# Hybrid decoder layer on one core: a written order for the first tile, readers of a PSUM bank grouped by engine, means on ScalarE, stores one step later

## The chip, the cores and the metric

The kernel runs on 1 core of a Trainium2 chip. The metric is the device time of one execution in microseconds (us). A core has five engines that each take their instructions in order and wait for one another by semaphores: TensorE (PE, matmuls and transposes), VectorE (DVE), ScalarE (ACT), GpSimd (POOL) and SyncE (SP), which here only issues DMAs. Matmuls write to PSUM; all other tiles lie in SBUF.

## The reference

One decoder layer on x of 1024 rows (tokens) by 1024 columns, all in float32:

```python
h = rms_norm(x, norm_mix_pre)
proj = h @ w_in                      # columns: u, v (256 each), then q, k, v of 12 heads (64 each)
a_out = spatial_gating(u, v, ...)    # gelu, layer norm of v, causal 128-row mix, times u
b_out = dilated_attention(q, k, v, rel_bias)
x = x + rms_norm(concat(a_out, b_out) @ w_out, norm_mix_post)
h = rms_norm(x, norm_ffn_pre)
g = gelu(causal_dwconv(h @ w_gate, conv_w, conv_b))
y = (g * (h @ w_up)) @ w_down        # 2816 inner columns
x = x + rms_norm(y, norm_ffn_post)
```

A norm is `x * rsqrt(mean(x*x) + eps) * gain`. In the kernel each is a sum of squares on ACT, a mean plus eps, the power −0.5 on POOL, and a multiplication on DVE.

## The kernel before

Rows are worked in 8 tiles of 128. Every matrix product in float32 is made of three passes with split operands: an operand is written as hi (a rounded copy) and lo (operand minus hi), and PE adds hi·hi, hi·lo and lo·hi. So each operand costs a copy (L77 on DVE, L73 on ACT; both are `split`) and a subtraction (L78, on DVE or POOL), and the names end in h and l: whuv and wluv are the weights for the columns u and v, hTh and hTl the transposed normed x, whv and wlv the first weights for the heads' v.

The stages, with their times in the profile:

- 0 to 25 us, the start: load of tile 0, its norm (`norm_x`), its transposes (`trans_x`, xT in PSUM), the split of four pieces of weight.
- to 75 us, the uv projection: for each tile 24 matmuls (`proj_a`), the transposes of the next tile in the middle of them (`mid`), and the gate's norm (`uv_a` to `uv_d`: tm, mu, mm, s, vnl). Between them the weights of the first head group are split (`split_w("v0", ...)`, for i = 3 to 6).
- to 148 us, the projections for the heads' v (`v_out`: hi on ACT, lo on DVE from a PSUM bank) and the gate's product.
- to 463 us, 12 heads. Projections of later heads (L479) fill PE between logits (s), softmax rows (row), transposes (pt, with the splits pth on ACT and ptl on DVE) and products with V (o). Late in it the finished columns of the first row tile are split for w_out (`mix_split`, tiles ms).
- to 552 us, w_out: for each tile in the order 0, 1, 2, 3, 4, 6, 5, 7 a product of 48 matmuls, then `wout_end` (squares, mean in two halves by `rstd_half`, norm, sum with x, and a second norm with `rstd_of`). The transposes of a finished tile (`h2_trans`, L728) stand on PE behind the product of the next one. Its eight scaled copies (L733, stg) and further splits (hs) are ACT's and DVE's.
- to 975 us, the gate and up products by a Strassen-Winograd scheme, with the convolution and gelu.
- to 1198 us, the down projection, in the same scheme: seven products, the steps (n, p), each with 11 pieces p. For every step an s tile is loaded (`sf`, L945) and split. In the last product (n = 4) the even row tiles are normed and stored (`final`, L1037 and L1038) while the odd ones are worked; the last five pieces are done for one odd tile after the other (the tail). L1059 is the add that ends a tile there, L1008 its square, L1023 its mean (n4m), L1025 its power.

The orders of PE and SP are as the code is written. DVE, ACT and POOL are ordered by a scheduler at build time, which places an instruction by its expected readiness, so the written order binds there only by its dependencies.

## Time and profile before

| what | value |
|---|---|
| median of 3 runs | 1198.22 us (1197.21 to 1200.38) |
| the profiled execution's own time | 1199.82 us |
| its span | 1198.1 us |
| PE busy | 1163.6 us, 97% |
| DVE, ACT, POOL busy | 839.7, 582.9, 370.6 us |
| PE idle | 34.5 us |

A row of the timeline has the start in us, the duration in us, the engine, the line, the operation and what it writes and reads; in brackets stands the idle time of the engine just before it and what ended that. Rows that follow each other with the same form are merged, with their count behind an x. The profile's lines are numbers of the kernel before; the kernel after has others (L1088 is the add of the tail, for instance).

### The profile page before, as it was taken

How to read it: one execution, taken by the hardware profiler on the slowest of the kernel's cores; microseconds unless marked ns; L12 is line 12 of the kernel's file. 1: busy time of each engine (PE TensorE's matmuls, PEld its weight loads, DVE VectorE, ACT ScalarE, POOL GpSimd, SP SyncE). 2: the span in 40 equal slices, each digit the busy share in tenths (PEclk: the TensorE clock that was granted, in tenths of full speed). 3: DMA queues.
4: the chain of work that ended last, by engine and by line, in shares of the span. 5: the costliest groups of instructions: out<-in, count | busy, mean ns of one | idle time of the engine just before them, and what ended most of it. 6: DMA issues, size and time to landing. Idle time of an engine off the chain costs nothing.

```text
span 1198.1 us, 16554 instructions
## 1 busy us (share of the span) xinstructions
PE 1163.6 (97%) x5691; PEld 976.8 (82%) x5691; DVE 839.7 (70%) x1559; ACT 582.9 (49%) x1174; POOL 370.6 (31%) x402
## 2 busy tenths in 40 slices
PE   7899999999999999999999999999999999999996
PEld 5789978888887878887788888888888888888884
DVE  5752257777777775468997678777777679779665
ACT  5532256667765664457534243432434345446521
POOL 2850023334323374234033313332133310000451
PEclk9999999999999999999999999999999999999998
DMA  5323133343233442251143323433143289334345
GB/s 180 106 59 89 25 83 73 91 117 84 73 78 76 108 141 71 92 173 53 36 132 97 115 67 117 132 97 106 62 132 106 88 302 357 97 97 129 110 130 203
DMA packets 107420, 134.31 MB, mean 112 GB/s; under 512 B 30779, under 2 KB 74311, under 8 KB 107336
## 3 DMA queue, kind: packets, MB, share of 16 engines
q1 hardware_dynamic: 105032, 131.15, 35.9%
q10 hardware_dynamic: 2304, 2.10, 0.5%
q8 instruction: 45, 0.74, 0.3%
q14 instruction: 39, 0.32, 0.1%
HBM read 98.30 MB, written 35.71 MB: 112 GB/s over the span
## 4 chain that ended last, share of the span: by engine, by line
PE 86%; DVE 5%; DMA 3%; POOL 2%; ACT 2%; issue 2%; SPq 0%; DVEq 0%; POOLq 0%; ACTq 0%
PE d L996 15%; PE qk L479 10%; PE y L630 7%; PE o L573 4%; PE pt L551 4%; PE s L519 2%; PE s L520 2%; PE v L242 2%; PE v L244 2%; PE v L243 2%; PE Bu L857 2%; PE Au L856 2%; PE Au L857 2%; PE Au L855 2%; PE Bu L856 2%; PE Bu L855 2%
## 5 line engine op out<-in xcount | busy, mean ns | idle before, releaser
L996 PE MATMUL d<-t,s 128*128 128x512 f32 x924 | 211.9, 391 | 1.9 <-ACT t L73 1.6
L996 PEld LDWEIGHTS d<-t,s 128*128 128x128 f32 x924 | 174.5, 189 | 39.2 <-ACT t L73 2.0
L531 POOL TENSOR_SCALAR row<-row,rz 128x128 f32<-128x128 f32 (+3 forms) x96 | 72.8, 759 | 213.2 <-DVE rz L530 200.2
L528 ACT ACTIVATE row<-row,nm 128x128 f32<-128x128 f32 (+3 forms) x96 | 74.4, 775 | 49.0 <-DVE nm L523 48.7
L556 DVE TENSOR_TENSOR ptl<-pt,pth 128x512 fp32r<-128x512 f32 (+1 forms) x120 | 75.7, 634 | 19.6 <-ACT pth L555 18.3
L630 PE MATMUL y<-woh,ms 128*128 128x512 f32 x256 | 82.8, 396 | 0.4 <-DVE Q L494 0.4
L555 ACT ACTIVATE pth<-pt 128x512 fp32r<-128x512 f32 (+1 forms) x120 | 65.8, 550 | 33.3 <-PE pt L551 31.9
L479 PE MATMUL qk<-hTh,wqh 128*128 128x512 f32 x192 | 81.1, 422 | 0.0
L73 ACT ACTIVATE s<-sf 128x512 fp32r<-128x512 f32 x77 | 48.2, 626 | 65.7 <-PE d L996 26.4
L479 PE MATMUL qk<-hTl,wqh 128*128 128x512 f32 x192 | 78.7, 410 | 0.0
L479 PE MATMUL qk<-hTh,wql 128*128 128x512 f32 x192 | 76.6, 399 | 0.0
L78 DVE TENSOR_TENSOR s<-sf,s 128x512 fp32r<-128x512 f32 x77 | 53.5, 695 | 24.0 <-ACT s L73 23.9
L551 PE MATMUL pt<-ident,row 128*128 128x128 f32 x432 | 68.4, 274 | 1.6 <-POOL row L531 1.5
L1011 POOL TENSOR_TENSOR x<-x,g4t 128x512 f32<-128x512 f32 x12 | 18.4, 1536 | 158.0 <-DMA g4t<-in_norm_ffn_post 133.8
L73 ACT ACTIVATE wtg<-tg 128x512 fp32r<-128x512 f32 x44 | 27.5, 632 | 80.9 <-PE Cu L857 67.8
L805 POOL TENSOR_TENSOR tu<-wu 128x512 f32<-128x512 f32 x11 | 17.5, 1590 | 156.1 <-PE Ag L857 74.5
L908 DVE SCALAR_TENSOR_TENSOR c<-G,cols,c 128x1023 f32<-128x1023 f32 (+1 forms) x44 | 57.7, 1329 | 6.7 <-ACT c L906 6.7
L523 DVE CUSTOM_DVE_ANT_0 row<-s,bias 128x384 f32<-128x384 f32 (+2 forms) x96 | 49.9, 519 | 17.7 <-PE s L520 11.8
L551 PEld LDWEIGHTS pt<-ident,row 128*128 128x128 f32 x432 | 51.3, 140 | 10.4 <-POOL row L531 2.5
L73 ACT ACTIVATE wtu<-tu 128x512 fp32r<-128x512 f32 x44 | 27.6, 630 | 64.2 <-PE Cg L857 50.8
L630 PEld LDWEIGHTS y<-woh,ms 128*128 128x128 f32 x256 | 47.9, 188 | 10.8 <-issue 0.8
L573 PE MATMUL o<-ptl,V 128*128 128x256 f32 x240 | 49.4, 287 | 4.8 <-DVE ptl L556 4.5
(329 smaller groups left out, 3232.5 us busy)
## 6 DMA issues: line engine op xcount, KB each, us to landing
sf<-sD SPq DMA_DIRECT2D x77, 256.0 KB, 2.8
wu<-in_w_up SPq DMA_DIRECT2D x11, 1024.0 KB, 5.0
wd<-in_w_down SPq DMA_DIRECT2D x22, 512.0 KB, 7.0
wg<-in_w_gate SPq DMA_DIRECT2D x10, 1024.0 KB, 6.0
sD<-c SPq DMA_DIRECT2D x30, 256.0 KB, 6.5
gcop<-gd SPq DMA_DIRECT2D x12, 576.0 KB, 4.8
wqk<-in_w_in SPq DMA_DIRECT2D x24, 256.0 KB, 6.0
bias<-gcop SPq DMA_DIRECT2D x12, 512.0 KB, 4.1
```

The source lines that it names most:

```text
L73: act.activation(hi, src, AF.Copy)
L78: lo_eng.tensor_sub(lo, src, hi.bitcast(F))
L479: pe.matmul(st[hf], w, m, start=k == 0 and j == 0, stop=k == KT - 1 and j == 2)
L528: act.activation(t[:, :w], t[:, :w], AF.Exp, bias=nm, scale=-1.0, accum_out=z)
L531: pool.tensor_scalar(t[:, :w], t[:, :w], rz, 1.0, op0=OP.mult, op1=OP.mult)
L551: pe.transpose(p[:, a * 128:(a + 1) * 128], r[:, jj * 128:(jj + 1) * 128], ident)
L555: act.activation(hi[:, :n], p[:, :n], AF.Copy)
L556: dve.tensor_sub(lo[:, :n], p[:, :n], hi.bitcast(F)[:, :n])
L573: pe.matmul(ov, v, t[:, s], start=j == 0 and x == 0, stop=x == 1 and j == 2 * g + 1, skip_group_check=True)
L630: pe.matmul(YP[i, hf], m, w, start=k == 0 and j == 0, stop=k == KT - 1 and j == 2)
L908: dve.scalar_tensor_tensor(c[:, d:T], g[:, 0:T - d], col(2 - d, f), c[:, d:T], op0=OP.mult, op1=OP.add)
L996: pe.matmul(b, l, r, start=first and n in FIRST and q == 0, stop=last and n in LAST and q == 2, skip_group_check=True)
```

## The change

It has seven parts.

1. The first block is put in a fixed order: on DVE, ACT and POOL what is written there is what runs. The gain row g1r is loaded on ACT's queue. Three matmuls on a tile of zeros (wz) are put ahead of the first true one. For the first weights hi goes to ACT, lo to DVE, and the normed tile 0 stands ahead of that lo on DVE. The norm of tile 1 moves into this block, in halves that read the gain from PSUM.
2. The mean plus eps is computed by ACT (an Identity with scale and bias) and no longer by POOL, in `rstd_of` with n = 1, in `rstd_half` and in `rstd_d`.
3. In `trans_x` and `v_out` the copies of hi by ACT come first for a whole PSUM bank, then the subtractions by DVE.
4. For i = 4 and 5 the lo part of the first v weights is DVE's, not POOL's.
5. The split of the first mixed tile (`mix_split` in the loop over heads) has hi on ACT and lo on POOL for all pieces; before, DVE had both for every other piece.
6. The stores of the even tiles are issued one step later, and the loads of the x1 tiles 1 and 3 earlier.
7. The tail multiplies by a copy of g4 in PSUM, made by ACT.

DVE around tile 5 of the uv projection, before (the number behind a name's first part is that of the tile: xT5_0 and xT5_1 are the two PSUM halves of tile 5's transposes, xn6 the normed tile 6; the last number is a serial one):

```order
L305 TENSOR_REDUCE s23_551<-tm3_492 128x4
L214 SCALAR_TENSOR_TENSOR xn6_504<-x6_433,n1_6r_509,g1t_98 128x1024
L78 TENSOR_TENSOR vnl0_188<-tm2_405,vnh0_186 128x256
L78 TENSOR_TENSOR hTl1_0_145<-xT5_0_533,hTh1_0_144 128x2x128
L78 TENSOR_TENSOR hTl1_2_149<-xT5_1_542,hTh1_2_148 128x2x128
L78 TENSOR_TENSOR hTl1_1_147<-xT5_0_533,hTh1_1_146 128x2x128
L78 TENSOR_TENSOR hTl1_3_151<-xT5_1_542,hTh1_3_150 128x2x128
```

and after:

```order
L322 TENSOR_REDUCE s23_566<-tm3_507 128x4
L78 TENSOR_TENSOR wlv01_532<-wv01_529,whv01_531 128x768
L241 TENSOR_TENSOR hTl1_0_153<-xT5_0_548,hTh1_0_152 128x2x128
L241 TENSOR_TENSOR hTl1_1_155<-xT5_0_548,hTh1_1_154 128x2x128
L221 SCALAR_TENSOR_TENSOR xn6_519<-x6_448,n1_6r_524,g1t_102 128x1024
L78 TENSOR_TENSOR vnl0_211<-tm2_420,vnh0_209 128x256
L241 TENSOR_TENSOR hTl1_2_157<-xT5_1_557,hTh1_2_156 128x2x128
L241 TENSOR_TENSOR hTl1_3_159<-xT5_1_557,hTh1_3_158 128x2x128
```

The subtraction for wlv01 came onto DVE, and the norm xn6 moved from ahead of all four hTl1 of tile 5 to the middle of them.

ACT in w_out at tile 6, before (yb6 with ssb6 is the square of a half of tile 6, n2_6m0 and n2_6m1 its two means, stg the copies of the transposes hT4 of the tile before, x2 for two instructions):

```order
L706 ACTIVATE yb6_6072,ssb6_6073<-y6_0_6022 128x512
L73 ACTIVATE ms7_0_6113<-mix1_776 128x128
L73 ACTIVATE ms7_0_6113<-mix3_2227 128x128
L73 ACTIVATE ms7_0_6113<-mix5_3545 128x128
L73 ACTIVATE ms7_0_6113<-mix7_4882 128x128
L706 ACTIVATE yb6_6072,ssb6_6073<-y6_1_6026 128x512
L73 ACTIVATE hs1_0_0_6133<-stg0_0_0_5644 128x2x256
L733 ACTIVATE stg0_0_0_5644<-hT4_0_6092,cols_84 128x128 x2
```

and after:

```order
L73 ACTIVATE ms7_0_6128<-mix7_4897 128x128
L161 ACTIVATE n2_6m0_6090<-ssb6_6088,epsc_81 128x1
L725 ACTIVATE yb6_6087,ssb6_6088<-y6_1_6041 128x512
L752 ACTIVATE stg0_0_0_5659<-hT4_0_6107,cols_88 128x128 x2
L752 ACTIVATE stg0_0_1_5660<-hT4_0_6107,cols_88 128x128 x2
L73 ACTIVATE hs1_0_0_6148<-stg0_0_0_5659 128x2x256
L752 ACTIVATE stg0_1_0_5670<-hT4_1_6116,cols_88 128x128 x2
L752 ACTIVATE stg0_1_1_5671<-hT4_1_6116,cols_88 128x128 x2
L161 ACTIVATE n2_6m1_6093<-ssb6_6088,n2_6m0_6090 128x1
```

The two means of the tile stand on ACT now (they were POOL's), the second behind the copies stg and one hs.

SP's queue in the last product, before (sf4_8 is the load for step 8 of the product n = 4, x1_2 the x1 tile for row tile 2, out a store of x12_0 and x6_0, the two halves of row tile 0):

```order
L945 DMA sf4_7_11150<-sD_88 128x512
L1030 DMA x1_2_11173<-x1d_85 128x1024
L1038 DMA out_0<-x12_0_10064 128x512
L1038 DMA out_0<-x6_0_10302 128x512
L945 DMA sf4_8_11183<-sD_88 128x512
L1030 DMA x1_4_11206<-x1d_85 128x1024
L1038 DMA out_0<-x12_1_10069 128x512
L1038 DMA out_0<-x6_1_10307 128x512
L945 DMA sf4_9_11216<-sD_88 128x512
```

and after:

```order
L964 DMA sf4_7_11165<-sD_92 128x512
L1049 DMA x1_2_11188<-x1d_89 128x1024
L964 DMA sf4_8_11196<-sD_92 128x512
L1057 DMA out_0<-x12_0_10079 128x512
L1057 DMA out_0<-x6_0_10317 128x512
L1049 DMA x1_4_11221<-x1d_89 128x1024
L964 DMA sf4_9_11229<-sD_92 128x512
L1057 DMA out_0<-x12_1_10084 128x512
L1057 DMA out_0<-x6_1_10322 128x512
L1049 DMA x1_6_11251<-x1d_89 128x1024
L964 DMA sf4_10_11259<-sD_92 128x512
```

The load for step 8 stands ahead of the first two stores now, and that for step 9 ahead of the second two; that for step 10 stands ahead of the third two, with the load of x1_6 ahead of it.

The diff, cut to its core:

```diff
@@ -129,6 +129,10 @@
+        epsc = cp.tile([128, 1], F, name="epsc")
+        pool.memset(epsc, EPS)
+        wz = cp.tile([128, 256], F, name="wz")
+        dve.memset(wz, 0.0)
@@ -142,7 +146,10 @@
         def rstd_of(ss, nm, n=1, width=float(D)):
...
-            pool.tensor_scalar(m, ss, 1.0 / width, EPS, op0=OP.mult, op1=OP.add)
+            if n == 1:
+                act.activation(m, ss, AF.Identity, scale=1.0 / width, bias=epsc)
+            else:
+                pool.tensor_scalar(m, ss, 1.0 / width, EPS, op0=OP.mult, op1=OP.add)
@@ -151,7 +158,7 @@
         def rstd_half(ss, hf, nm):
...
-            pool.tensor_scalar(m, ss[:, hf:hf + 1], 1.0 / D, HM.pop(nm) if hf else EPS, op0=OP.mult, op1=OP.add)
+            act.activation(m, ss[:, hf:hf + 1], AF.Identity, scale=1.0 / D, bias=HM.pop(nm) if hf else epsc)
@@ -200,11 +207,11 @@
-            if i == 0:
+            if i < 2:
...
-                    r = rstd_half(ss, hf, "n1_0")
+                    r = rstd_half(ss, hf, "n1_%d" % i)
@@ -214,7 +221,7 @@
-        def trans_x(i):
+        def trans_x(i, mid=None):
@@ -226,10 +233,14 @@
+                pv = [p[:, j * 256:(j + 1) * 256].rearrange("p (k c) -> p k c", k=2) for j in range(2)]
+                h = [[hT[i // 4, 2 * q + j, w][:, :, s] for w in range(2)] for j in range(2)]
...
-                    pv = p[:, j * 256:(j + 1) * 256].rearrange("p (k c) -> p k c", k=2)
-                    hi, lo = hT[i // 4, 2 * q + j, 0][:, :, s], hT[i // 4, 2 * q + j, 1][:, :, s]
-                    split(hi, lo, pv, act, dve)
+                    act.activation(h[j][0], pv[j], AF.Copy)
+                for j in range(2):
+                    dve.tensor_sub(h[j][1], pv[j], h[j][0].bitcast(F))
+                if q == 0 and mid is not None:
+                    mid()
...
         def proj_a(key, n, i, nm, mid=None):
@@ -245,22 +256,28 @@
-        load_x(0)
-        sp.dma_start(g1r[0:1, :], bass.AP(tensor=g1.tensor, offset=g1.offset, ap=[[D, 1], [1, D]]))
-        G1 = [bP("g1_%d" % hf) for hf in range(2)]
-        for hf in range(2):
-            s = slice(hf * 512, (hf + 1) * 512)
-            pe.matmul(G1[hf], ones, g1r[0:1, s], start=True, stop=True)
-        for kp in range(4):
-            load_w("uv", 0, 512, kp)
-        load_x(1)
-        norm_x(0)
-        for hf in range(2):
-            act.activation(g1t[:, hf * 512:(hf + 1) * 512], G1[hf], AF.Copy)
-        split_w("uv", 512, 0, dve, dve)
-        trans_x(0)
-        for kp in range(1, 4):
-            split_w("uv", 512, kp, act if kp % 2 else dve, dve)
+        wb = bO("wb")
+        with tc.manual_schedule(engines={ET.DVE, ET.Activation, ET.Pool}):
+            act.dma_start(g1r[0:1, :], bass.AP(tensor=g1.tensor, offset=g1.offset, ap=[[D, 1], [1, D]]))
+            load_x(0)
+            for kp in range(4):
+                load_w("uv", 0, 512, kp)
+            load_x(1)
+            for _ in range(3):
+                pe.matmul(wb[:, :256], wz[:, :128], wz, start=True, stop=True)
+            G1 = [bP("g1_%d" % hf) for hf in range(2)]
+            for hf in range(2):
+                s = slice(hf * 512, (hf + 1) * 512)
+                pe.matmul(G1[hf], ones, g1r[0:1, s], start=True, stop=True)
+            norm_x(0)
+            split_w("uv", 512, 0, act, dve)
+            trans_x(0, lambda: split_w("uv", 512, 1, act, dve))
+            split_w("uv", 512, 2, act, dve)
+            split_w("uv", 512, 3, act, dve)
+            norm_x(1)
+            for hf in range(2):
+                act.activation(g1t[:, hf * 512:(hf + 1) * 512], G1[hf], AF.Copy)
...
         def load_rows():
@@ -329,7 +346,6 @@
-                norm_x(1)
@@ -341,7 +357,7 @@
                 load_w("v0", C0["v"], 384, i - 3)
-                split_w("v0", 384, i - 3, act, pool)
+                split_w("v0", 384, i - 3, act, dve if i in (4, 5) else pool)
             def mid():
@@ -384,14 +400,17 @@
         def v_out(vg, i, p):
+            vt, src = [], []
...
-                vt = V[pr_, i // 4].rearrange("p (t x c) -> p t x c", t=4, x=4)[:, i % 4]
-                src = p[:, j * 128:(j + 1) * 128].rearrange("p (x c) -> p x c", x=2)
-                act.activation(vt[:, 0:4:3, :], src, AF.Copy)
-                dve.tensor_sub(vt[:, 1:3, :], src, vt.bitcast(F)[:, 0:4:3, :])
+                vt.append(V[pr_, i // 4].rearrange("p (t x c) -> p t x c", t=4, x=4)[:, i % 4])
+                src.append(p[:, j * 128:(j + 1) * 128].rearrange("p (x c) -> p x c", x=2))
+            for v, a in zip(vt, src):
+                act.activation(v[:, 0:4:3, :], a, AF.Copy)
+            for v, a in zip(vt, src):
+                dve.tensor_sub(v[:, 1:3, :], a, v.bitcast(F)[:, 0:4:3, :])
@@ -611,11 +630,11 @@
-        def mix_split(i, mh, ml, ks):
+        def mix_split(i, mh, ml, ks, engs=None):
...
-                split(mh[:, k], ml[:, k], src, act if k % 2 else dve, pool if k % 2 else dve)
+                split(mh[:, k], ml[:, k], src, *(engs or ((act, pool) if k % 2 else (dve, dve))))
@@ -655,7 +674,7 @@
-                        mix_split(0, m0[0], m0[1], range(KT - 1))
+                        mix_split(0, m0[0], m0[1], range(KT - 1), (act, pool))
@@ -1018,9 +1037,9 @@
-                pool.tensor_scalar(m, SS[i][:, a:a + 1], 1.0 / D, EPS, op0=OP.mult, op1=OP.add)
+                act.activation(m, SS[i][:, a:a + 1], AF.Identity, scale=1.0 / D, bias=epsc)
...
-            pool.tensor_scalar(m, SS[i][:, b:b + 1], 1.0 / D, SM[i], op0=OP.mult, op1=OP.add)
+            act.activation(m, SS[i][:, b:b + 1], AF.Identity, scale=1.0 / D, bias=SM[i])
@@ -1029,13 +1048,23 @@
+        STO = []
+        def stores():
+            while STO:
+                i, s, y = STO.pop(0)
+                sp.dma_start(out[i * 128:(i + 1) * 128, s], y)
...
         def final(i, ys):
...
-                (act if i == NT - 1 and hf else sp).dma_start(out[i * 128:(i + 1) * 128, s], y)
+                if i % 2:
+                    (act if i == NT - 1 and hf else sp).dma_start(out[i * 128:(i + 1) * 128, s], y)
+                else:
+                    STO.append((i, s, y))
...
         def evac_d(n, m):
@@ -1168,6 +1197,9 @@
         late = [p for p in range(LS + 2)]
...
+            if n == 4 and p in (5, 6):
+                load_x1(1 if p == 5 else 3)
+            stores()
             ahead_s(x_ + LS)
@@ -1196,15 +1228,15 @@
             if n == 4 and 2 <= p < 6:
...
-        load_x1(1)
-        load_x1(3)
+        gp = bS("g4p")
+        act.activation(gp, YG["g4"][:, 0:512], AF.Copy)
...
             for p in range(NP - NL, NP):
...
             evac_d(4, m)
...
-            dve.tensor_mul(xt("1", m), xt("1", m), YG["g4"][:, 0:512])
+            dve.tensor_mul(xt("1", m), xt("1", m), gp)
```

## The prediction

> **What bounds the kernel now.** I read the page first, then the table of busy time by stage, then the list of what TensorE waited for, and last the timeline around each of those waits.
>
> ```profile
> PE 1163.6 (97%) x5691; PEld 976.8 (82%) x5691; DVE 839.7 (70%) x1559; ACT 582.9 (49%) x1174; POOL 370.6 (31%) x402
> ```
>
> TensorE (PE) is busy for 97% of the span, and the change takes no matmul out of it. What can be won is the idle time, 1198.1 − 1163.6 = 34.5 us, and the time in which PE is busy at a lower clock. The rows of six stages (columns: stretch, its length, then the busy time of PE, of its weight load, of VectorE (DVE), ScalarE (ACT) and GpSimd (POOL), the granted TensorE clock, and DMA) show where they lie.
>
> ```profile
> 25.00:75.00 50.00, 46.69 (x223) 38.59 (x222) 35.09 (x74) 22.84 (x60) 40.08 (x52) 0.97 0.29 91
> ...
> 350.00:375.00 25.00, 22.32 (x126) 19.10 (x125) 18.18 (x49) 15.09 (x36) 8.87 (x12) 0.93 0.33 82
> ...
> 463.00:552.00 89.00, 89.00 (x425) 73.92 (x424) 49.97 (x112) 45.28 (x144) 31.88 (x67) 1.00 0.38 125
> 552.00:600.00 48.00, 43.53 (x187) 35.05 (x186) 44.07 (x69) 31.44 (x55) 10.45 (x7) 0.96 0.10 34
> ...
> 1140.00:1177.40 37.40, 35.51 (x153) 28.86 (x153) 23.33 (x31) 10.19 (x22) 14.27 (x14) 0.98 0.54 173
> 1177.40:1198.10 20.70, 11.27 (x45) 8.86 (x44) 11.02 (x16) 2.89 (x8) 5.22 (x8) 0.83 0.45 158
> ```
>
> PE idles 50.00 − 46.69 = 3.31 us in the uv projection, 2.68 us in 25 us of the heads, 4.47 us where the gate and up products begin, 1.89 us late in the down projection and 9.43 us in the tail. In w_out (463 to 552) it idles not at all. Where PE idled the clock column falls too: 0.03 × 50 = 1.5 us, 0.07 × 25 = 1.75 us, 0.04 × 48 = 1.9 us, 0.02 × 37.4 = 0.75 us. So a stall costs about half as much again as the list of waits says (line, releaser: us in total, times, longest):
>
> ```profile
> PE o L573 <- DVE ptl L556: 4.5, 3, 2.7
> ...
> PE Eg L856 <- DVE hs L78: 2.6, 1, 2.6
> ```
>
> The longest of each is one event with one place. The change touches the first, and the waits in the uv projection, late in the down projection, at the start and in the tail (below). It does not touch the Eg wait: nothing is reordered there, so that stage's 4.47 us and its clock stay.
>
> **The start (parts 1 and 2 of the change).**
>
> ```profile
> 11.35 0.78 PE L242 MATMUL uv<-whuv,hTh 128*128 128x512 f32 x1
> ...
> 15.19 0.61 PE L244 MATMUL uv<-whuv,hTl 128*128 128x512 f32 x1
> 15.63 0.39 PE L242 MATMUL uv<-whuv,hTh 128*128 128x512 f32 x1
> 15.86 0.40 PE L243 MATMUL uv<-wluv,hTh 128*128 128x512 f32 x1
> ...
> 19.09 1.10 PE L227 MATMUL xT<-ident,xn 128*128 128x128 f32 x8 [1.19 <-DVE xn L214]
> ...
> 24.23 1.03 PE L227 MATMUL xT<-ident,xn 128*128 128x128 f32 x8
> ```
>
> ```profile
> 11.29 1.06 ACT L73 ACTIVATE whuv<-r 128x1024 fp32r<-128x1024 f32 x1
> ...
> 15.66 1.05 ACT L212 ACTIVATE xn<-x 128x1024 f32<-128x1024 f32 x1
> ...
> 22.14 1.28 ACT L293 ACT_TABLE_LOAD   x1
> ```
>
> Before, the hi and lo parts of the first weights stand on DVE ahead of the normed tile 0. After, hi is ACT's and lo stands behind the norm, and I put the first uv matmul 2 to 3 us ahead of 11.35. This is not yet the gain, since tile 1 must follow. Its squares stand on ACT behind the fourth weight copy. The second copy that ACT made before ended at 11.29 + 1.06 = 12.35, and I take that for the fourth. From tile 1's square to its transposes it took 19.09 − 15.66 = 3.43 us; in halves, with a mean more, some 3.9: near 16.3 in place of 19.09. Then comes what is late next: the order on DVE has tile 2's norm behind the mean mu of tile 0's gate values, and that waits for the table load and the gelu behind it. The six matmuls of tile 0 that follow tile 1's transposes are done near 18.5; the load (1.28), the gelu and mu (0.4 each) and the norm (1.29, the row of the next part) follow: tile 2's transposes near 22.3 against 24.23. I take −1.9; the ends are −0.5 (the loads set the pace, not the order) and −3.0 (tile 1's lead is kept whole). The three dummy matmuls and the earlier load of the gain row run where PE waits for data; if that cover were gone, they would cost 2 us of the same lead.
>
> **The uv projection, tile 5 (part 4).**
>
> ```profile
> 19.75 1.29 DVE L214 SCALAR_TENSOR_TENSOR xn<-x,n_2r,g1t 128x1024 f32<-128x1024 f32 x1 [0.71 <-POOL n_2r L147]
> ...
> 48.25 1.80 POOL L78 TENSOR_TENSOR wlv<-wv,whv 128x768 fp32r<-128x768 f32 x1
> 48.32 2.82 DVE L214 SCALAR_TENSOR_TENSOR xn<-x,n_6r,g1t 128x1024 f32<-128x1024 f32 x1 [0.49 <-ACT whv L73]
> ...
> 51.86 0.50 PE L244 MATMUL uv<-whuv,hTl 128*128 128x512 f32 x1 [3.31 <-DVE hTl L78]
> ```
> The same norm takes 1.29 us alone and 2.82 beside POOL's wlv, and the four hTl that PE waits for stand behind it. After, this wlv is on DVE, at 768 / 1024 × 1.29 = 0.97 (an estimate), and two of the four hTl stand ahead of the norm. DVE does 0.97 more and saves 1.53. The stall of 3.31 and its clock loss of 1.5 go: 4.8 us. DVE now has two such splits (i = 4 and 5) among 35.09 us of work in 50, and the next norm stands behind the second; I leave 0.5 for what they delay: −4.3, ends −2.5 (half the stall comes back, at tile 7) and −4.8. The regrouping itself (part 3) changes only which of hi and lo comes second; beside the v projections PE has no wait, so I cost it at nothing there, 0.4 a tile (one split) if the cover were gone.
>
> **The heads (part 5).**
>
> ```profile
> 365.15 1.30 POOL L78 TENSOR_TENSOR ms<-mix,ms 128x128 fp32r<-128x128 f32 x3
> ...
> 366.58 2.84 DVE L78 TENSOR_TENSOR ms<-mix,ms 128x128 fp32r<-128x128 f32 x3
> 366.62 2.65 POOL L78 TENSOR_TENSOR wql<-wqk,wqh 128x512 fp32r<-128x512 f32 x2 [0.17 <-ACT wqh L73]
> ```
>
> Three low parts cost DVE 2.84 beside POOL's wql, and ptl, for which PE waits, is behind them. After, DVE has none: the six casts are ACT's, the six subtractions POOL's at 1.30 / 3 = 0.43 each, done about 1.3 us later than its three were, with two rows of the softmax and wql behind them. ACT has 9.9 us free of 25. The stall of 2.68 and the clock's 1.75 go, less some 0.9 for ptl's second piece, now behind a row of the next block, and for POOL's row: −3.5, ends −2.2 and −4.4.
>
> **The means in w_out (part 2), the cost.**
>
> ```profile
> 484.57 0.75 DVE L716 TENSOR_SCALAR xb<-yb,n_1r 128x1024 f32<-128x1024 f32 x1 [2.13 <-POOL n_1r L147]
> ...
> 488.35 1.03 PE L728 MATMUL hT<-ident,xb 128*128 128x128 f32 x8
> ...
> 525.68 2.17 ACT L733 ACTIVATE stg<-hT,cols 128x128 f32<-128x128 f32 x8
> ...
> 527.67 1.41 DVE L710 SCALAR_TENSOR_TENSOR yb<-y,n_6r,g2t 128x512 f32<-128x512 f32 x2 [0.44 <-POOL n_6r L159]
> ...
> 534.54 0.75 DVE L716 TENSOR_SCALAR xb<-yb,n_6r 128x1024 f32<-128x1024 f32 x1 [0.72 <-POOL n_6r L147]
> ...
> 535.47 1.03 PE L728 MATMUL hT<-ident,xb 128*128 128x128 f32 x8
> ```
>
> On POOL the second mean of a tile ran as soon as its square was done. On ACT it stands, in the order, behind the eight copies, and at tile 6 behind one hs copy (some 0.6) as well: 525.68 + 2.17 + 0.6 = 528.4, and with the mean (0.3) and the power (0.55, as in the tail) DVE can start at 529.3 in place of 527.67, 1.6 later. DVE also puts one operation of 0.7 more ahead of the add. The normed tile was done at 534.54 + 0.75 = 535.29, 0.18 ahead of PE's need: 1.5 to 2.3 us become a stall. Tile 1 was done 3.0 us ahead of its transposes, and there the same delay is hidden. A stall of this size may lower the clock: the 1.89 us of idle time up to 1177.4 did, since the tail's matmuls (below) average 431 ns.
>
> ```profile
> L996 PE MATMUL d<-t,s 128*128 128x512 f32 x47 | 12.5, 431 | 0.3 <-DVE t L78 0.3
> ...
> L1023 POOL TENSOR_SCALAR n4m<-ssd,n4m 128x1 f32<-128x1 f32 x4 | 3.0, 756 | 20.2 <-ACT jk L1008 20.2
> ```
>
> The rows at 15.19 and 15.63 have 0.61 at the low clock and 0.39 at the full one, so 47 × 0.041 / 0.22 = 9 of them ran slowly, at 0.2 each (0.43 against 0.23 from start to start) 1.8 us. [...] I take +2.6 (1.9 of stall and half of a clock loss of 1.5), ends 0 (the third norm's mean, now on ACT too, wins the time back) and +4.0.
>
> **Late down projection (part 6).**
>
> ```profile
> 1141.97 0.42 SPq L1030 DMA_DIRECT2D x<-x1d  x1
> 1159.55 1.01 SPq L1038 DMA_DIRECT2D out<-x  x2
> 1160.66 0.40 SPq L945 DMA_DIRECT2D sf<-sD  x1
> ```
>
> The last row is the load of the s tile of step 8. It stood on SP's queue behind the stores of 1159.55, which waited for DVE. After, the load stands directly behind the row of 1141.97, some 18 us earlier, and the loads of steps 9 and 10, each behind one pair of stores less, by a few us. The stall of 1.89 and 0.75 of clock go in part. What is late next is the last norm of an even tile: its x1 load is behind stores, and the splits of steps 9 and 10 stand behind it on DVE. I take −1.9, ends −1.0 and −2.6.
>
> **The tail (parts 2 and 7).** Four times, one after the other: add, square, mean, power, two DVE halves, next add. The first and the last of the four adds are
>
> ```profile
> 1177.41 0.69 DVE L1059 TENSOR_TENSOR x<-d,x 128x512 f32<-128x512 f32 x1 [1.31 <-PE d L996]
> ...
> 1190.51 0.69 DVE L1059 TENSOR_TENSOR x<-d,x 128x512 f32<-128x512 f32 x1
> ```
>
> so a round takes 13.10 / 3 = 4.37 us, where PE needs 15 × 0.23 = 3.4. The mean on POOL is 0.756 (row above) beside DVE's product with g4. In its place stands one ACT operation of 128x1. Two rows bound it:
>
> ```profile
> L733 ACT ACTIVATE stg<-hT,cols 128x128 f32<-128x128 f32 x64 | 17.5, 392 | 0.0
> ...
> L73 ACT ACTIVATE ms<-mix 128x128 fp32r<-128x128 f32 x32 | 7.2, 298 | 0.0
> ```
>
> A pointer operand adds 94 ns, and 128 columns are worth about 107 (1024 columns take ACT 1.05, the row at 15.66), so 0.29 (an estimate). And ACT starts it 0.1 earlier, as it is behind its own square. The product now reads PSUM, which keeps it out of POOL's way. Saved: 0.756 − 0.29 + 0.1 = 0.57 to 0.66 a round, four rounds: −2.4, ends −1.2 (the mean takes twice the estimate) and −2.8. The copy of g4 into PSUM lies beside PE's work.
>
> **Sum.** −1.9 − 4.3 − 3.5 + 2.6 − 1.9 − 2.4 = −11.4 us. The profiled execution took 1199.82 us (1.7 outside its span), 1.6 above the median of 1198.22. 1199.82 − 11.4 = 1188.4, less 1.6: about 1187.
>
> **The rivals.**
>
> *Covered again.* DVE and ACT take their instructions in order, and each removed stall is replaced by a shorter one behind it: tile 2's norm behind mu, the two wlv on DVE, the last norm behind its x1. For it: DVE is 70% busy, and ahead of each stall it was one operation that came late. Against it: the removed stalls come from operations stretched to more than twice, and the stretch goes. All the small ends: −0.5 − 2.5 − 2.2 + 4.0 − 1.0 − 1.2 = −3.4, so 1194.8.
>
> *Slower: ACT's queue in w_out.* The second mean behind the copies delays every tile and not only tile 6. PE is at 89.00 of 89.00 there, so each microsecond beyond the slack is a microsecond of the end. It decides from the point at which a tile's chain is over 3 us later; seven tiles at 2 us each beyond that, with the clock, are 14 + 3 = 17 against the 14 won elsewhere: 1201. For it: ACT's copies are on the way of the next tile's add too, so delays can add up from tile to tile. Against it: by the order only 2.2 to 2.8 us of copies are ahead of a mean, and ACT is busy for 45.28 of 89.
>
> *The clock at the start.* The dummy matmuls run from about 1 us, so PE could be at the full clock by its first uv matmul. Before, ten matmuls run at 0.43 in place of 0.23 between 11.35 and 15.63. With those 2.0 us gone and the upper ends of the other terms, it is −1.9 − 2.0 − 4.8 − 4.4 + 1.0 − 2.6 − 2.8 = −17.5: 1180.7. For it: PE has work in more of the first 8 us. Against it: PE waited for tile 1 before (1.19 at 19.09), and a faster PE waits for it longer. [...]
>
> **How the numbers follow.** Forecast (two thirds or more of the stalls go, tile 6 pays) 0.62; covered again 0.19; slower 0.06; clock at the start 0.13. The ends of the sum are 1180.7 and 1194.8; a little beyond the upper one, for a second stall like that of tile 6, the range is 1180.5 to 1195.5. It leaves out the slower case and the outer tails, 2 in 10. A difference under 0.3% (3.6 us: between 1194.6 and 1201.8) can't be told from none. The covered case lies on that edge: of its 0.19, 0.09 is faster. So faster is 0.62 + 0.13 + 0.09 = 0.84, the same 0.10 and, with the heavy part of the third case, slower 0.06.
>
> **What would show it.** In the profile after: no PE wait near tile 5 of uv, xn there at 1.3 us; no wait of o for ptl over 1 us in the ninth head; PE idle in w_out, 1.5 to 2.3 us at tile 6's transposes, where there was none; sf for step 8 issued near 1142; the adds of the tail every 3.8 us. A PE idle time of over 5 us in w_out, or stalls as long as before in the uv stage, would make it wrong.

## The result, and the profile after

The changed kernel takes 1192.22 us, median of 6 runs (1190.69 to 1193.57); the kernel before, beside it, 1198.93 (6 runs, 1195.30 to 1200.38). The ratio is 0.9945, 95% interval 0.993 to 0.996: faster by 0.55%. The profiled execution has a span of 1191.2 us against 1198.1, so 6.9 us are to be explained where 11.4 were forecast. The first line of the page after:

```profile
PE 1162.8 (98%) x5697; PEld 975.0 (82%) x5697; DVE 832.0 (70%) x1553; ACT 593.1 (50%) x1233; POOL 351.0 (29%) x356
```

PE idles 1191.2 − 1162.8 = 28.4 us in place of 34.5: 6.1 us of the gain is idle time; the other 0.8 is shorter busy time (the clock, 0.996 for 0.992 over the span, less the three added matmuls, 2.9 at the start). The stages after, with one (75 to 148) that the forecast left out (columns as in the prediction):

```profile
25.00:75.00 50.00, 50.00 (x251) 41.85 (x251) 37.83 (x82) 24.24 (x65) 37.40 (x46) 1.00 0.29 92
75.00:148.00 73.00, 70.00 (x390) 66.92 (x389) 17.94 (x57) 15.01 (x56) 8.28 (x6) 0.98 0.21 58
...
350.00:375.00 25.00, 24.53 (x149) 21.27 (x150) 18.05 (x50) 17.91 (x42) 10.99 (x16) 1.00 0.37 87
...
463.00:552.00 89.00, 87.89 (x416) 72.96 (x415) 49.63 (x101) 50.34 (x159) 24.16 (x43) 1.00 0.36 119
552.00:600.00 48.00, 43.01 (x184) 34.21 (x183) 42.37 (x66) 28.68 (x49) 12.18 (x7) 0.96 0.10 32
```

The uv stage and the heads are nearly whole. A new gap of 3.00 us stands in 75 to 148, with the clock at 0.98; before, the same stretch was

```profile
75.00:148.00 73.00, 72.40 (x412) 68.90 (x412) 21.27 (x60) 19.89 (x58) 11.28 (x9) 1.00 0.22 58
```

The same events on PE (on DVE for the add), read from both traces, give a ledger. The stage column is what each stage alone won or lost; it sums to −6.9.

| up to this event | before | after | stage | forecast |
|---|---|---|---|---|
| transposes of tile 2 | 24.23 | 23.21 | −1.0 | −1.9 |
| uv matmul behind tile 6's transposes | 56.68 | 50.40 | −5.3 | −4.3 |
| bias matmul behind the first gate products | 87.54 | 84.89 | **+3.6** | 0 |
| projection after the ninth head | 374.13 | 368.06 | −3.4 | −3.5 |
| first transposes in w_out | 476.56 | 471.44 | +0.9 | 0 |
| transposes of tile 7 in w_out | 559.03 | 556.97 | +3.1 | +2.6 |
| a Bg product behind the Eg wait | 579.14 | 576.21 | −0.9 | 0 |
| first add of the tail | 1177.41 | 1172.91 | −1.6 | −1.9 |
| end of the span | 1198.1 | 1191.2 | −2.4 | −2.4 |

What TensorE waits for after the change:

```profile
PE o L592 <- DVE ptl L575: 3.4, 3, 1.9
PE z L426 <- DVE u L430: 3.0, 4, 2.0
PE Eg L875 <- DVE hs L78: 2.0, 1, 2.0
PE hT L747 <- ACT hs L73: 1.5, 1, 1.5
...
PE hT L747 <- DVE xb L735: 1.1, 1, 1.1
```

The z wait (z is the gate's product, mix times v; u its result) and the two hT waits are new. The longest o wait, 1.9, is at 432.44 in the heads, where before there was one of 0.82:

```profile
430.96 0.43 DVE L77 CAST woh<-wo 128x512 fp32r<-128x512 f32 x1 [2.11 <-DMA wo<-in_w_out]
...
432.44 0.51 PE L592 MATMUL o<-ptl,V 128*128 128x256 f32 x2 [1.90 <-DVE ptl L575]
```

DVE waits there for a load of w_out's weights, with ptl behind it. Now the z wait. In the timeline after, around it:

```profile
73.62 1.56 ACT L73 ACTIVATE whv<-wv 128x768 fp32r<-128x768 f32 x2
74.53 1.82 POOL L78 TENSOR_TENSOR wlv<-wv,whv 128x768 fp32r<-128x768 f32 x1 [1.26 <-ACT whv L73]
75.22 1.95 DVE L78 TENSOR_TENSOR wlv<-wv,whv 128x768 fp32r<-128x768 f32 x1 [1.04 <-ACT whv L73]
77.09 0.47 DVE L430 SCALAR_TENSOR_TENSOR u<-z,cols,u 128x256 f32<-128x256 f32 x1
...
77.61 0.39 PE L426 MATMUL z<-vnh,wT 128*128 128x256 f32 x1 [2.05 <-DVE u L430]
```

ACT makes two copies back to back, so POOL and DVE begin to subtract almost together, each from two SBUF tiles. DVE's takes 1.95, u is behind it, and z has two PSUM buffers, so the third z product waits for u. POOL came first: it ends at 74.53 + 1.82 = 76.35, and a full DVE subtraction (0.94, a row of the first experiment) after that ends at 77.29; the measured end is 77.17. Within 0.12, that is what it would be if DVE did nothing until POOL was through.

In w_out, after (DVE unless ACT or PE is named; yb and xb are the normed sum and the normed tile):

```profile
522.77 0.35 ACT L161 ACTIVATE n_6m<-ssb,n_6m 128x1 f32<-128x1 f32 x1
...
524.28 1.40 DVE L729 SCALAR_TENSOR_TENSOR yb<-y,n_6r,g2t 128x512 f32<-128x512 f32 x2
...
530.85 0.75 DVE L735 TENSOR_SCALAR xb<-yb,n_6r 128x1024 f32<-128x1024 f32 x1 [1.03 <-POOL n_6r L154]
531.66 1.09 PE L747 MATMUL hT<-ident,xb 128*128 128x128 f32 x8 [1.11 <-DVE xb L735]
```

Tile 6's second mean comes at 522.77, behind eight stg copies and an hs, and the first yb 1.5 later, behind the power and two operations of DVE; the normed xb is done at 531.60, and PE pays 1.11. At tile 7 the row of PE names ACT's hs, which ended 0.05 behind the normed tile xb; but the transposes read xb, and start 0.14 behind its end, as they do in e1 (0.15), where the row names xb. And xb waited for POOL:

```profile
549.26 0.75 DVE L788 TENSOR_TENSOR hsum<-stg,stg 128x256 f32<-128x256 f32 x2
549.49 6.04 POOL L827 TENSOR_TENSOR tg<-wg,tg 128x512 f32<-128x512 f32 x1 [2.67 <-DVE tg L825]
551.91 0.36 ACT L150 ACTIVATE n_7m<-ssc,epsc 128x1 f32<-128x1 f32 x1
555.48 0.55 POOL L154 TENSOR_TENSOR n_7r<-n_7m,half 128x1 f32<-128x1 f32 x1
556.07 0.76 DVE L735 TENSOR_SCALAR xb<-yb,n_7r 128x1024 f32<-128x1024 f32 x1 [1.70 <-POOL n_7r L154]
556.97 1.07 PE L747 MATMUL hT<-ident,xb 128*128 128x128 f32 x8 [1.52 <-ACT hs L73]
```

POOL's tg, 1.35 us in the profile of before, takes 6.04: DVE ran its subtractions and sums one behind the other until 554.4, and tg came through only then (554.2 + 1.35 = 555.5); the power n_7r, whose mean was there at 552.3, stood behind it.

Late in the down projection and in the tail:

```profile
1168.27 1.41 DVE L1063 SCALAR_TENSOR_TENSOR x<-x,n4r,x 128x512 f32<-128x512 f32 x2 [1.97 <-DMA x<-x1d]
...
1170.94 0.97 PE L1015 MATMUL d<-t,s 128*128 128x512 f32 x3 [0.56 <-DVE t L78]
...
1172.91 0.69 DVE L1088 TENSOR_TENSOR x<-d,x 128x512 f32<-128x512 f32 x1 [0.82 <-PE d L1015]
...
1184.28 0.68 DVE L1088 TENSOR_TENSOR x<-d,x 128x512 f32<-128x512 f32 x1
```

The last even norm (tile 6) waits 1.97 for its x1 load, and PE 0.56 and then 0.24 for the splits behind it, where 1.89 of idle time stood before. A round of the tail is (1184.28 − 1172.91) / 3 = 3.79 against 4.37.

### The profile page after: what moved, and what is told of

It reads as the page before. It is cut to its first block, busy times and chain, and to the rows that moved or that the text cites. A ratio compares the mean times of both kernels' runs of the same rounds, so it can differ in the third digit from the quotient of the medians.

```text
span 1191.2 us, 16581 instructions
## 1 busy us (share of the span) xinstructions
PE 1162.8 (98%) x5697; PEld 975.0 (82%) x5697; DVE 832.0 (70%) x1553; ACT 593.1 (50%) x1233; POOL 351.0 (29%) x356
## 4 chain that ended last, share of the span: by engine, by line
PE 82%; issue 4%; ACT 4%; POOL 4%; DVE 4%; DMA 1%; DVEq 0%; POOLq 0%; ACTq 0%; SPq 0%
PE d L1015 15%; PE qk L498 10%; PE y L649 5%; PE o L592 4%; PE pt L570 4%; PE s L538 2%; PE s L539 2%; PE v L253 2%; PE Bu L876 2%; PE v L254 2%; PE v L255 2%; PE Bu L874 2%; PE Bu L875 2%; PE Au L876 2%; PE Cu L876 2%
## 5 line engine op out<-in xcount | busy, mean ns | idle before, releaser
L78 DVE TENSOR_TENSOR s<-sf,s 128x512 fp32r<-128x512 f32 x77 | 57.1, 741 | 21.1 <-ACT s L73 21.0
```

## The experiments

Each kernel is the changed one with one edit; where not told otherwise it is one run, its span is set against 1191.2 of the changed kernel, and "sooner" and "later" compare the same event in these two.

**e1, grouping in the v projections undone** (part 3 in `v_out`).

```diff
-            for v, a in zip(vt, src):
-                act.activation(v[:, 0:4:3, :], a, AF.Copy)
-            for v, a in zip(vt, src):
-                dve.tensor_sub(v[:, 1:3, :], a, v.bitcast(F)[:, 0:4:3, :])
+                act.activation(vt[:, 0:4:3, :], src, AF.Copy)
+                dve.tensor_sub(vt[:, 1:3, :], src, vt.bitcast(F)[:, 0:4:3, :])
```

> The changed kernel with v_out alone written as before: hi on ACT and lo on DVE piece by piece. In the changed kernel PE waits 2.0 us and 0.36 us for u in the first gate product (z, near 77 us), and from there the lead over the kernel before falls from 6.3 to 2.7 us. Theory A (the grouping let the order on ACT put two weight copies whv back to back behind vnh, so that POOL's and DVE's low parts wlv run at the same time and both stretch, with u behind DVE's): this run has whv, vnh, whv on ACT again, DVE's wlv takes under 1.2 us in place of 1.95, the wait of z for u is under 0.6 us, the lead after z stays above 5 us, and the span is about 3 us under the 1191.2 of the changed kernel. Theory B (PE merely reaches z 6 us sooner and the v1 weights do not come sooner; the grouping has no part in it): the wait at z stays at 1.5 us or more and the span is within 1 us of 1191.2.

1191.4 us (before beside it 1199.1), span 1189.4. DVE ahead of u:

```profile
74.00 1.78 DVE L78 TENSOR_TENSOR vnl<-tm,vnh 128x256 fp32r<-128x256 f32 x1 [0.84 <-ACT vnh L73]
75.69 0.94 DVE L78 TENSOR_TENSOR wlv<-wv,whv 128x768 fp32r<-128x768 f32 x1
```

ACT's copies come in the order of before (whv, vnh, whv), and POOL's wlv now lies beside vnl (1.78, where it takes 0.42 alone, at 73.75 in the changed kernel) and not beside DVE's wlv (0.94 for 1.95). That is how it was before the change too:

```profile
78.79 1.84 POOL L78 TENSOR_TENSOR wlv<-wv,whv 128x768 fp32r<-128x768 f32 x1
...
79.14 1.77 DVE L78 TENSOR_TENSOR vnl<-tm,vnh 128x256 fp32r<-128x256 f32 x1 [0.84 <-ACT vnh L73]
```

But there PE came to z late enough to wait only 0.38; here the wait is 1.33, in place of 2.05, and the clock stays full. Theory A had it under 0.6, theory B had it unchanged; neither holds whole. At the bias matmul the kernel is 2.5 us sooner, at 972 us 3.65, and at the end 1.8: late in the down projection tile 6's norm waits 3.74 for its x1 load and PE 2.46. So the grouping is a part of the z loss, not all of it, and a gain upstream is half lost late.

**e2, the second v weights wholly on POOL.**

```diff
-            split_w("v1", 384, kp, act, dve if kp % 2 else pool)
+            split_w("v1", 384, kp, act, pool)
```

> The changed kernel with all four low parts of the second group of v weights (wlv for v1) on POOL, where two of the four were on DVE. The order on ACT is that of the changed kernel, so the two copies whv stay back to back. Theory A (the collision of POOL's wlv and DVE's wlv holds u): DVE has no wlv there, u starts within 0.5 us of z's first product, the wait of z for u is under 0.6 us, the span about 3 us under 1191.2. Theory B (PE comes sooner than the weights and everything else): u does not need the weights, so by B, too, u is free; but then the v product of the next group would wait for its weights, 1 us or more at L253 to L255 near 100 us, and less than 2 us of the 3.6 are won.

1191.1 us, span 1188.9.

```profile
75.07 3.62 POOL L78 TENSOR_TENSOR wlv<-wv,whv 128x768 fp32r<-128x768 f32 x2 [1.26 <-ACT whv L73]
75.79 0.48 DVE L430 SCALAR_TENSOR_TENSOR u<-z,cols,u 128x256 f32<-128x256 f32 x1 [1.07 <-PE z L428]
```

The two subtractions follow each other on POOL, nothing of DVE stands behind them, u waits for its z and no z waits over 0.44. The bias matmul is 2.8 us sooner with the grouping in place. So the pair of wlv is the cause of the long wait, and the grouping acts by bringing the pair together.

The time from the bias matmul ahead of z to the one behind it leaves out what came earlier: 11.6 us before, 15.2 after the change, 12.5 in e1, 11.9 in e2. In e5, e7 and e10 (below), which have the same collision but kept the full clock, it is 13.6. So of the 3.6 us lost here 2.1 are waits, nearly all of which the pair makes, and 1.6 are a clock that fell.

**e3, the means in w_out back on POOL** (part 2 in `rstd_half`, and for the third norm).

```diff
-            if n == 1:
+            if n == 1 and nm[:2] != "n3":
...
+            if nm[:2] == "n2":
+                pool.tensor_scalar(m, ss[:, hf:hf + 1], 1.0 / D, HM.pop(nm) if hf else EPS, op0=OP.mult, op1=OP.add)
```

> The changed kernel with the means of the two norms in w_out back on POOL (n2 halves and n3); the means at the start, in the uv projection and in the down projection stay on ACT. In the changed kernel PE waits 1.1 us at the transposes of tile 6 (for the normed tile) and 1.5 us at those of tile 7 (for ACT's hs copy), and the lead falls by 3.1 us from 451 to 559 us. Theory of the prediction (the mean on ACT stands behind the copies stg and hs): both waits go, w_out has no PE idle time again as in the kernel before, and the span is about 3 us under 1191.2 (from 2.0 to 3.5). Rival (the later arrival of the tiles comes from elsewhere, for instance from the other order of DVE at tile 6): the wait at tile 6 stays over 0.7 us and the span is within 1.5 us of 1191.2.

1190.78 us, span 1189.1.

```profile
463.00:552.00 89.00, 89.00 (x422) 74.28 (x421) 50.98 (x104) 48.32 (x142) 30.86 (x63) 1.00 0.36 119
```

PE is whole again, and both hT waits are gone. From the first transposes (470.22) to tile 7's (552.70) it takes 82.5 us, as before (82.5), where the change takes 85.5: the whole +3.1 is the means. The Eg wait behind it is longer (2.6 for 2.0), and the x1 load of tile 6 is waited for again (3.06): of 4.3 us at tile 7 (1.2 of them were there ahead of w_out already, where its code is the same), 2.1 are left at the end.

**e4, the first v weights back on POOL** (part 4 undone).

```diff
-                split_w("v0", 384, i - 3, act, dve if i in (4, 5) else pool)
+                split_w("v0", 384, i - 3, act, pool)
```

> The changed kernel with all four low parts of the first v weights (wlv for v0) on POOL again, as before. Theory of the prediction (the stall at tile 5 of the uv projection, 3.3 us and 1.5 us of clock, came from the norm of tile 6 being stretched from 1.29 to 2.82 us beside POOL's wlv, with hTl behind it): the norm takes over 2.2 us again, PE waits 2 us or more for hTl or xT between 40 and 60 us, and the span is 3 to 5 us over 1191.2. Rival (the new place of the norm behind two of the four hTl, which the grouping in trans_x brings, is enough by itself): the norm is stretched, but PE waits less than 1 us there and the span is within 1.5 us of 1191.2.

1199.0 us, span 1196.8: 5.6 longer, of the 6.9 that the change brings.

```profile
46.05 1.28 DVE L221 SCALAR_TENSOR_TENSOR xn<-x,n_6r,g1t 128x1024 f32<-128x1024 f32 x1
46.15 2.90 POOL L78 TENSOR_TENSOR wlv<-wv,whv 128x768 fp32r<-128x768 f32 x1
47.25 2.08 DVE L78 TENSOR_TENSOR vnl<-tm,vnh 128x256 fp32r<-128x256 f32 x1
...
58.54 1.09 PE L234 MATMUL xT<-ident,xn 128*128 128x128 f32 x8 [1.57 <-DVE xn L221]
```

The norm was expected to be stretched again and is not. The two still meet, but now the norm comes first: wlv waits for it (until 47.33, 1.2 of its 2.90), vnl waits for wlv (2.08, for 0.42 at 58.73 of this run), and the stall, shorter, appears at tile 7. Only 2.4 us are lost there and the rest later, to 3.65 at 972 and 2 more in the last stages. The pair is again the cause; which side of it suffers turned on a tenth of a microsecond.

**e5, the tail's mean back on POOL, the product still from PSUM.**

```diff
-                act.activation(m, SS[i][:, a:a + 1], AF.Identity, scale=1.0 / D, bias=epsc)
+                pool.tensor_scalar(m, SS[i][:, a:a + 1], 1.0 / D, EPS, op0=OP.mult, op1=OP.add)
...
-            act.activation(m, SS[i][:, b:b + 1], AF.Identity, scale=1.0 / D, bias=SM[i])
+            pool.tensor_scalar(m, SS[i][:, b:b + 1], 1.0 / D, SM[i], op0=OP.mult, op1=OP.add)
```

> The changed kernel with the mean of the down projection's norms (n4m) back on POOL; the product of the tail still reads the copy of g4 in PSUM. In the tail a round from add to add is 4.37 us before and 3.79 us in the changed kernel. Theory of the prediction (what counts is that ACT makes the mean, right behind its own square): with POOL the mean costs its old 0.76 us or at least 0.5 with the wait, a round is 4.2 us or more and the four rounds give 1.6 us or more back. Rival (what stretched the mean from 0.19 to 0.76 us was the product reading two tiles of SBUF on DVE; with one of them in PSUM POOL's mean is 0.19 again): POOL's n4m takes under 0.25 us in the tail, a round is 3.7 to 3.9 us, and the end moves by less than 0.5 us.

1189.33 us (before 1198.17), span 1187.4. The group of the mean, and the first and last add:

```profile
L1042 POOL TENSOR_SCALAR n4m<-ssd,n4m 128x1 f32<-128x1 f32 x4 | 1.1, 264 | 17.5 <-ACT jk L1027 17.5
```

```profile
1168.84 0.69 DVE L1088 TENSOR_TENSOR x<-d,x 128x512 f32<-128x512 f32 x1 [1.29 <-PE d L1015]
...
1180.33 0.68 DVE L1088 TENSOR_TENSOR x<-d,x 128x512 f32<-128x512 f32 x1
```

With the product out of the way POOL's mean takes 0.264, not 0.756, and the round is 11.49 / 3 = 3.83, 0.04 from the change's. (The kernel is quicker ahead of the tail, where its scheduler puts tile 6's norm behind two splits and nothing waits for x1; 1.6 us of its lead is a clock that stayed full, below.)

**e6, the mean on ACT, the product from SBUF as before.**

```diff
-            dve.tensor_mul(xt("1", m), xt("1", m), gp)
+            dve.tensor_mul(xt("1", m), xt("1", m), YG["g4"][:, 0:512])
```

> The changed kernel with the tail's product reading g4 from SBUF as before (the copy in PSUM is made and not used); the mean stays on ACT. If the mean on ACT is what saves: a round is still 3.8 to 3.9 us. If the PSUM operand is what saves: the power on POOL (0.55 us) now runs beside the product and is stretched to 0.8 us or more, and a round is 4.1 us or more, so that the end comes 1 us or more later than in the changed kernel.

1196.49 us, span 1194.6.

```profile
L1044 POOL TENSOR_TENSOR n4r<-n4m,half 128x1 f32<-128x1 f32 x4 | 2.8, 712 | 25.3 <-ACT n4m L1042 25.3
```

Now the power waits for the product: 0.712 for 0.549 of the change. The rounds are 4.74 (an add that waited 0.72 for PE, just behind a stall for x1), 3.95 and 3.93, between the two expectations. The first round is long in other runs that stall ahead of it too (4.50 before, 5.03 in e4), so I compare the second and third alone: 4.30 before, 3.80 after the change, 3.81 in e5, 3.94 here. Of the 0.50 that such a round won, the operand in PSUM alone brings 0.49 and ACT's mean alone 0.36. With ACT's mean alone POOL's power is left beside the product and takes 0.16 more; with the operand in PSUM alone (e5) its mean takes 0.264 and its power 0.55.

**e7, the even stores issued at once** (part 6 undone in part).

```diff
-                if i % 2:
+                if True:
```

> The changed kernel with the stores of the even tiles issued at once again (undoes the deferral in part 6; the loads of the x1 tiles 1 and 3 stay at their earlier place). Theory of the prediction (the s loads of steps 8 to 10 stood behind stores that wait for DVE): step 8's load is issued behind the first stores again, PE waits 1.5 us or more for the s tiles of the last two steps, and the time from step 0 of the last product to the first add of the tail is 1.2 to 2.2 us longer than in the changed kernel. Rival (the end of that stage hangs on the norm of tile 6, which waits for its x1 load, and the splits behind it on DVE, whatever the order of the stores): the first add of the tail moves by less than 0.6 us.

1194.88 us, span 1192.8.

```profile
1158.92 0.38 SPq L964 DMA_DIRECT2D sf<-sD  x1
...
1168.69 1.42 DVE L1063 SCALAR_TENSOR_TENSOR x<-x,n4r,x 128x512 f32<-128x512 f32 x2 [2.51 <-DMA x<-x1d]
...
1171.37 0.97 PE L1015 MATMUL d<-t,s 128*128 128x512 f32 x3 [2.03 <-DVE t L78]
```

The load for step 8 is again behind two stores (the row of 1158.92), but no long wait of PE hangs on it: it has landed at 1161.59, and PE's first wait of this stage is the 2.03 at 1171.37, for a split behind tile 6's norm, which waits 2.51 for its x1 load. That is the mechanism of the rival, though not its size. From 972 us to the first add this run takes 203.0 us against 201.0 of the change. The same stretch takes 202.6 before, and 200.6 to 202.9 in the eight other runs that keep both the deferral and this stage's means on ACT (e1 to e4, e6, e8 to e10). There it goes with the wait for x1: 1.7 us of wait and 200.6 in e10, 2.5 and 201.7 in e4, 3.7 and 202.9 in e1. This run is 1.2 us longer than e4, with the same wait; more than that is not shown for the deferral.

**e8, the mixed tile's split as before** (part 5 undone).

```diff
-                        mix_split(0, m0[0], m0[1], range(KT - 1), (act, pool))
+                        mix_split(0, m0[0], m0[1], range(KT - 1))
```

> The changed kernel with the split of the first mixed tile as before (DVE has hi and lo of every other piece; undoes part 5). Theory of the prediction (three low parts on DVE are stretched beside POOL's wql, and ptl is behind them): DVE's three subtractions take 2 us or more, PE waits 2 us or more for ptl near 365 us, the clock falls there, and the span is 3 to 4.5 us over 1191.2. Rival (the collision was one of that moment: PE and the weights' arrival stand 2.7 us differently now, so that the subtractions miss wql): PE waits less than 1 us and the span is within 1 us of 1191.2.

1197.38 us, span 1195.3.

```profile
364.48 2.84 DVE L78 TENSOR_TENSOR ms<-mix,ms 128x128 fp32r<-128x128 f32 x3
364.50 2.67 POOL L78 TENSOR_TENSOR wql<-wqk,wqh 128x512 fp32r<-128x512 f32 x2
```

The wait of o for ptl is back at 2.7, though the clock stays full here (1.00 in 350 to 375, 0.93 before). At the projection behind the ninth head the kernel is 2.5 us later than the change (0.2 of it was there ahead of the stall), at tile 7 in w_out 1.8, and at the end 4.1.

**e9, without the three dummy matmuls.**

```diff
-            for _ in range(3):
-                pe.matmul(wb[:, :256], wz[:, :128], wz, start=True, stop=True)
```

> The changed kernel without the three dummy matmuls at the start (and without their tile of zeros). Rival of the prediction (the dummies raise the clock): in the changed kernel the uv matmuls are at full rate (0.23 us from start to start) from 10.9 us on, 1.4 us after the first of them; without the dummies they stay at 0.43 us for 3 us or more after the first, and tile 2's transposes come 0.5 us or more after 23.21. Theory of the prediction (PE waits for tile 1 and tile 2 in any case, so that the clock in these 3 us is worth little): tile 1's transposes stay at 16.3 and tile 2's at 23.2, each within 0.3 us, and the dummies are worth nothing that reaches the end.

1193.26 us (before 1199.72, median of 11), span 1191.3.

```profile
10.66 0.39 PE L251 MATMUL uv<-whuv,hTh 128*128 128x512 f32 x1
```

The uv matmuls follow each other at the full rate (0.23 from start to start) from 10.66 on without the dummies and from 10.89 on with them, and tile 2 is 0.25 sooner without. One run cannot tell what they do to the clock: in the runs that keep them this time lies anywhere from 10.9 to 15.0 (e8, with the clock at 0.86 in 0 to 25). But tile 2's transposes lie between 23.2 and 24.1 in all of these, at 23.40 in e8 and at 23.21 in the change, so an earlier full clock hardly reaches them.

**e10, grouping in `trans_x` undone for tiles 2 to 7** (the rest of part 3).

```diff
+                if i < 2:
...
+                else:
+                    for j in range(2):
+                        split(h[j][0], h[j][1], pv[j], act, dve)
```

> The changed kernel with trans_x piece by piece as before for the tiles 2 to 7 (hi on ACT, lo on DVE; undoes half of part 3). If the grouping has a part in the uv gain (two of tile 5's hTl stand ahead of the norm only because of it): the four hTl stand behind the norm or each waits for its own copy, and PE loses 0.5 to 2 us between 25 and 75 us where the changed kernel loses nothing. If the move of wlv to DVE is all of it: PE is busy for 50.0 of 50.0 us there again and the lead at 70 us is within 0.5 us of the changed kernel's.

1192.2 us, span 1190.3.

```profile
PE uv L259 <- DVE hTl L78: 0.9, 1, 0.9
```

PE is 1.3 us later at tile 6's transposes and 1.6 later at the bias matmul ahead of z (71.30 for 69.68): this grouping is worth that in the uv stage. It is not lost at z, where both wait 2.05: the bias matmul behind z is at 84.93 for 84.89 only because the clock fell in the change's profile and not here. In e5 and e7, where it did not fall either, it is at 83.27 and 83.31.

**e11, a version from the findings**: the edits of e2, e3 and e5 in one, shown there.

```diff
-            split_w("v1", 384, kp, act, dve if kp % 2 else pool)
+            split_w("v1", 384, kp, act, pool)
...
+            if nm[:2] == "n2":
...
+            pool.tensor_scalar(m, SS[i][:, b:b + 1], 1.0 / D, SM[i], op0=OP.mult, op1=OP.add)
```

> The changed kernel with three things set right by the runs so far: the means of w_out and of the down projection on POOL (at the start and in the uv projection they stay on ACT), and all low parts of the second group of v weights on POOL. From the runs apart: w_out 3 us less, z 2 to 3 us less, the wait late in the down projection (0.7 and 0.4 us with the clock) gone as in the run with the tail's mean on POOL. If these add, the time is 1183 to 1186 us, a ratio of 0.987 to 0.990 to the kernel before. If a later wait takes part of it, as the run with w_out's means on POOL lost 1.3 of its 3.4 us late in the down projection, it is 1187 to 1189.

1186.61 us (median of 6, 1185.93 to 1188.27), ratio to before 0.9898 (0.9881 to 0.9915), span 1185.1.

```profile
75.00:148.00 73.00, 71.77 (x405) 68.09 (x404) 14.66 (x55) 14.87 (x56) 11.89 (x8) 1.00 0.23 58
```

PE is also at 89.00 of 89.00 in w_out. The kernel is 3.3 us sooner behind z, 5.8 at tile 7, 5.0 at 972, and has no late x1 wait, as in e5. It beats both kernels: its median is 5.6 us below the changed one's, and the intervals of the two ratios do not meet. The time lies between the two ranges that were expected: most of the three gains add, not all.

**e12, e11 with the even x1 loads a step earlier.**

```diff
+            if n == 4 and p < 4:
+                load_x1(2 * p)
...
-            if n == 4 and 1 <= p < 5:
-                load_x1(2 * (p - 1))
```

> The kernel of the run before this one, with the loads of the even x1 tiles issued one step earlier, ahead of the stores of the step. If the end of the down projection hangs on the norm of tile 6 waiting for its x1 load with the splits of the last steps behind it: DVE no longer waits for that load (it waited 2.0 us in the changed kernel and 3.1 and 3.7 us in two of the runs), and the time is 0.5 to 2 us under the run before. If that wait is already gone with the order that the mean on POOL gives: the same time within 0.5 us.

1186.31 us (1185.95 to 1187.22), ratio 0.9895 (0.9876 to 0.9913): no difference from e11, where the wait that it would remove is gone already.

## Why the prediction was right or wrong

The direction and the range held; the point was 5 us too low. In the profiles the gain is 6.9 for 11.4, and 3.6 of the 4.5 between them are one term, that of the v projections. By its steps:

- **uv, tile 5** (−4.3): right in cause and near in size, −5.3. Undoing part 4 loses 2.4 in this stage, through another victim, and 5.6 at the end (e4). Undoing the grouping in `trans_x`, which I costed at nothing, loses 1.6 (e10). The two do not sum to the 5.3, so how it divides is not shown.
- **The heads** (−3.5): right, −3.4. Undoing it gives back 2.3, with a clock that stays full (e8); the rest goes with the clock, which fell here before (0.93).
- **w_out** (+2.6): right in sign and near in size, +3.1, all of it the means (e3). The stall at tile 6 was to be 1.5 to 2.3 and is 1.1; that tile 7 has a second one was missed. The half of a clock loss in the +2.6 was my estimate, and this profile does not show it: the clock is 1.00 in 463 to 552. In e1 and in e4 to e10 that second wait is 0.8 and tg takes 1.35, so 0.7 of the 1.5 belongs to the tg of 6.04, which comes in the profile of after and in e2 only; in those other runs the stage costs 2.4.
- **Late down** (−1.9): −1.6, near in size by luck, as far as these runs show. What was named as late next, tile 6's norm behind its x1 load, is late, and with its wait this stage moves by 2.3 us between runs with the same code here; for the deferral alone the runs show no more than 1.2 (e7). The forecast also began with the load of step 8, but what PE waited for before was a split behind that of step 10, issued at 1168.45:

```profile
1174.14 0.63 ACT L73 ACTIVATE s<-sf 128x512 fp32r<-128x512 f32 x1 [3.55 <-DMA sf<-sD]
```

- **The tail** (−2.4): the size was right and the reason half of it. I gave the saving to ACT's shorter mean; keeping the product's operand out of SBUF alone does as much as both (0.49 of the 0.50 of a round, e5), and ACT's mean alone less (0.36, e6).
- **The failed step is "The regrouping itself … beside the v projections PE has no wait, so I cost it at nothing there, 0.4 a tile".** True of before, but the order of ACT's copies sets when POOL and DVE subtract, and PE came there 6.3 us sooner. It cost 3.6: 2.1 of waits and, in executions where the clock falls behind them, 1.6 of clock. e1 and e2 show the cause of the waits; it is a collision of the kind that the term for tile 5 removed, one stage on.
- **The start** (−1.9): −1.0. I had tile 2 at 22.3 behind mu; it is at 23.21. The order of the terms was right (mu at 21.45, then the norm, then the transposes), with each a little later than estimated. The rival on the clock falls, by the argument that stood against it: with the full rate from 10.66 (e9), 10.89 (the change) or 15.0 (e8), tile 2's transposes start at 22.96, 23.21 and 23.40. (Its sum also took +1.0 for w_out, where the best end stated was 0.)
- Not costed at all: +0.9 late in the heads, where PE waited 1.90 at 432.44 for ptl against 0.82 before. A load of w_out's weights landed 5.7 us after its issue there against 3.5 before. In all runs the wait goes with the time of that load (e9: 4.1 us and 0.81; e2: 5.1 and 1.34; e7: 5.6 and 1.87), though their code here is the same, so this is a matter of the execution; why the load is slower than before in all of them stays open. And −0.9 at Eg, where the stall is 2.0 for 2.6; it is 2.6 again in e3, e11 and e12, in which PE does not wait at tile 7 just ahead of it.

So "covered again" described a part of it: what is won early is partly waited for again, at z and at x1, but the removed stalls stayed removed.

## What to carry to other kernels

After a reordering, list each pair of a POOL instruction and a DVE instruction that read only SBUF and may now fall together, and look at what stands behind the later one: in the pairs seen here it took 1.95 for 0.94 (DVE's wlv), 1.78 for 0.42 (vnl), 2.82 for 1.29 (xn6) and 2.90 for 1.80 (wlv on POOL). Removing one such pair can bring PE sooner to the next, as it did at z, 6.3 us sooner. Before an operation is moved to another engine because it is slow, find what makes it slow: the tail's mean took 0.756 with the product's g4 in SBUF and 0.264 with it in PSUM (e5), and in w_out the move cost more than it saved. Where PE is busy all the time, look at what a small operation would stand behind: in w_out, with PE at 89.00 of 89.00 before, tile 6's second mean (0.35) stood on ACT behind the copies from 520.25 to 522.77, and PE waited 1.11. And before a stage's time in one run is put down to that run's edit, look at the same stage in the runs that left it alone.
